# First mixer of a two-layer decoder: the solve's steps are placed at other places between the products, and the next group's mixes run beside them

## The chip, the core and the metric

The kernel runs on one core of one Trainium2 chip. Its time is the device time of one execution in microseconds (µs), and the number that stands for a kernel is the median of several executions. A core has five engines with a queue of their own each: TensorE (PE in the profile, its weight loads are PEld), VectorE (DVE), ScalarE (ACT), GpSimd (POOL) and SyncE (SP, which here only issues copies between memories). Each engine works through its queue in order and waits on semaphores that others raise.

## The reference, cut to what matters

Two layers, 256 positions, 2048 channels. The first layer's mixer is a gated delta rule with 32 value heads on 16 key heads of width 128; the change touches it alone.

```python
proj = x @ w_in                                   # 256 x 2048 by 2048 x 12352
qkv, z, a, b = split(proj)
q, k, v = split(silu(causal_dwconv(qkv, conv_w))) # 16, 16 and 32 heads of 128
q, k = l2norm(q) * 128**-0.5, l2norm(k)
beta, g = sigmoid(b), -exp(a_log) * softplus(a + dt_bias)
# per head, in chunks of 64: decay from the cumulated g
sol = triangular_solve(I + strict(kb @ k.T * decay), [v * beta, kb * exp(gc)])
# a scan over the chunks carries the state S
o = (q * exp(gc)) @ S + tri(q @ k.T * decay) @ v_new
o = o * rsqrt(mean(o**2) + eps) * norm_g * silu(z)
y = o.reshape(256, 4096) @ w_o
```

After it come a layer norm, a gated convolution block, a second norm, a gated side input, and the second layer with another mixer. All matrices are float32.

## The kernel before, in words

**Products.** Every large product takes float32 weights in tiles of 512 KB (`raw`, four buffers, issued by SP at L110). ACT rounds a tile to a shorter format (`hi`, L115) and DVE takes the rest (`lo`, L116), three buffers each. A product then needs three passes, of the rounded weights with both halves of the input and of the rest with the rounded input. Keys, queries and values come out transposed through `gemm_t_steps` (L148 for `hi`, L152 for `lo`, results in `mm_ps`): a tile is 8 products with `hi` and 8 with `lo`. The gate z comes from `gemm_steps` (L187, L190, L194, results in `b_ps`): a tile is 12 products.

**Groups.** The first mixer goes in eight groups of two key heads and four value heads. For a group the stream of products is 8 tiles of values, 8 tiles of the next group's keys and queries, and 8 tiles of the next group's z, 24 tiles in all. In the last group the output weights stand in for what no next group needs (`ahead`).

**Small work of a group.** Beside the stream, each group needs a row of small products in plain float32, which the profile lists as two passes each:

- `front`: the keys with themselves (`g_ps<-k`, L546 and L547, the first small work after a group's z). From them DVE makes `L` (L582), copies bring `L` to memory and back (`lt`, `ld`), POOL inverts the diagonal blocks with them. The masked products `gt` (L511) use the buffer of `L` again, so they wait until the copies `lt<-L` have landed.
- `solve`: forward substitution in four blocks (index b) for each half of the positions (a = 0, 1). A step is `l_ps` (L708, products with the blocks before), `ts` (L710, DVE), `y_ps` (L714), `ys` and four `u` (L716, L718, ACT). Between the halves stand `x_ps` (L695), a DVE step into `v` (L697) and the transposes `v_ps` (L668).
- `outputs`: `o_ps` (L732, L733), squares on ACT, a reciprocal root and the gate on DVE; its transposes `ot_ps` (L752) are put off through the list `rest`.
- `mixes`: the queries with the keys (`g_ps<-q,k`), `qd` and `qo` (L599, L600, DVE), sums `ss_ps` (L606) and scales `s_ps` (L612).

**What sets the order.** `solve`, `outputs` and `mixes` are generators. `finish` chains them and is kept in `self.inter`; the products of `gemm_t_steps` call `next(self.inter)` after every second `hi` row and at the end of each half tile, so 24 times in 8 tiles. `gemm_steps` calls it after every row of products too. A bare `yield` is thus a place between products. What is left of `self.inter` when it is needed is written out at once. The framework's scheduler then orders each engine's queue by its own estimate of when things are ready; a small product can so stand a few products away from where it was written. In PSUM two banks (`sp`) serve `g_ps`, `ss_ps`, `s_ps` and one half of `v_ps`, two more (`bk`) `l_ps`, `y_ps`, `x_ps`, `o_ps`, `ot_ps` and the other half; a bank is given out again when its readers are done.

Of the kernel before, what the change touches and what calls it, by code (L numbers as in the profile page):

```python
# [2 lines left out]

# [62 lines left out]
class Trunk:  # L66
# [382 lines left out]
    def gdn_groups(self, pool, gk, cw, ng, oT, load, gates, ahead):  # L449
# [12 lines left out]
        for pd in pads:  # L462
            nc.gpsimd.memset(pd[:, 0:3], 0.0)
        h4 = range(4)
        five = lambda ap: ap.rearrange("p (j r) t -> p j r t", r=2)

        def conv(n0, out):
# [126 lines left out]
        def mixes(s):  # L594
            q, k, dm = (s[x] for x in ("q", "k", "qd"))

            p1, p2 = gram(k, q)
            for a, ps in enumerate((p1, p2)):
                nc.vector.tensor_tensor(five(dm[:, a]), bcast(ps[:, :, 0:P], 2, 2), five(dm[:, a]), op=ALU.mult)  # L599
            nc.vector.tensor_tensor(five(s["qo"]), bcast(p1[:, :, P:S], 2, 2), five(s["qo"]), op=ALU.mult)  # L600
            yield

            pss = self.sp.tile([P, 4], F32, tag="sp", name="ss_ps")
            for h in range(2):
                for a in range(2):
                    nc.tensor.matmul(pss[:, 2 * h + a:][:, 0:1], s["sq"][:, h, a * P:(a + 1) * P],  # L606
                                     self.ones[:, 0:1], start=True, stop=True)
            xm = pool.tile([P, 4, 16], F32, tag="xm", name="xm")
            nc.vector.tensor_tensor(xm, bcast(s["x8"].rearrange("p q e -> p (q e)"), 4, 1), bcast(self.blk, 16, 2),
                                    op=ALU.mult)  # L610
            ps8 = self.sp.tile([P, 16, 4], F32, tag="sp", name="s8_ps")
            nc.tensor.matmul(ps8.rearrange("p e h -> p (e h)"), self.rep, xm.rearrange("p b e -> p (b e)"),  # L612
                             start=True, stop=True)
            xh = pool.tile([P, 16, 4], F32, tag="xm", name="xh")
            nc.vector.tensor_tensor(xh, ps8, bcast(self.blk, 16, 1), op=ALU.mult)
            s8 = s["s8"] = pool.tile([P, 4, 2, 2], F32, tag="s8", name="s8", bufs=2)
            nc.vector.tensor_reduce(s8.rearrange("p b q a -> p (b q a)"), xh, axis=mybir.AxisListType.X, op=ALU.add)
            wq = s["wq"] = pool.tile([P, 2, 2], F32, tag="wq", name="wq", bufs=2)
            nc.vector.tensor_scalar(wq.rearrange("p h a -> p (h a)"), pss, 4 * RMS_EPS, RMS_EPS * 128.0,
                                    op0=ALU.add, op1=ALU.mult)  # L620
            rr = pool.tile([P, 2, P], F32, tag="y0", name="rr")
            nc.sync.dma_start(out=rr, in_=bass.AP(tensor=s["rd"].tensor, offset=s["rd"].offset,
                                                  ap=[[0, P], [P, 2], [1, P]]))
            nc.vector.tensor_tensor(five(s["n21"]), bcast(rr, 2, 2), five(s["n21"]), op=ALU.mult)
# [51 lines left out]
        def zgate(s, rest):  # L676

            zs = s["zs"] = pool.tile([P, 2, 512], F32, tag="zs", name="zs", bufs=2)

            def done(a, ps):  # L680
                nc.scalar.activation(zs[:, a], ps, AF.Tanh, scale=0.5)
                nc.vector.scalar_tensor_tensor(zs[:, a], zs[:, a], 1.0, ps, op0=ALU.add, op1=ALU.mult)

            for j, _ in enumerate(self.gemm_steps(w_in, 8192 + 512 * s["g"], 512, lambda k: self.xT[:, k], KT, done)):
                if j > 4 and rest:
                    rest.pop(0)()

        def solve(s):
            u = s["u"] = pool.tile([P, 2, 4, P], F32, tag="u", name="u")
            bank = lambda name: self.sp.tile([P, P], F32, tag="bk", name=name)  # L690
            for a in range(2):
                if a:
                    ps = self.sp.tile([P, 4, 4, 32], F32, tag="bk", name="x_ps")
                    for h in h4:
                        nc.tensor.matmul(ps[:, :, h], u[:, 0, h], s["n21"][:, h].rearrange("p (b i) -> p b i", b=4),  # L695
                                         start=True, stop=True)
                    nc.vector.scalar_tensor_tensor(s["v1"], ps, -2.0, s["v1"], op0=ALU.mult, op1=ALU.add)  # L697
                    yield
                    yield
                    s["turn"](1)  # L700
                    yield
                y = pool.tile([P, 4, P], F32, tag="y", name="ys", bufs=2)
                for b in range(4):
                    r = s["vs"][:, b]
                    if b:
                        ps = bank("l_ps")
                        for c in range(b):
                            nc.tensor.matmul(ps, LB[:, a, pair(c, b)], y[:, c], start=not c, stop=c == b - 1)  # L708
                        r = pool.tile([P, P], F32, tag="ts", name="ts")
                        nc.vector.scalar_tensor_tensor(r, ps, s["s8"][:, b, 1, a:a + 1], s["vs"][:, b],  # L710
                                                       op0=ALU.mult, op1=ALU.add)
                        yield
                    ps = bank("y_ps")
                    nc.tensor.matmul(ps, pm[:, a, b], r, start=True, stop=True)  # L714
                    if b < 3:
                        nc.scalar.activation(y[:, b], ps, AF.Copy)  # L716
                    for h in h4:
                        nc.scalar.activation(u[32 * b:32 * b + 32, a, h], ps[32 * h:32 * h + 32], AF.Copy)  # L718
                    yield
                yield  # L720

        def outputs(s):

            g, u = s["g"], s["u"]
# [3 lines left out]
            for a in range(2):  # L728
# [8 lines left out]
                nc.vector.scalar_tensor_tensor(f[:, a], ss[:, a], 1.0 / 128, bcast(s["wq"][:, :, a], 2, 2),  # L737
                                               op0=ALU.mult, op1=ALU.add)
                parts.append(ps)
                yield  # L740
            fa = self.rsqrt(pool, f.rearrange("p a j r -> p (a j r)"), 8)

            def gate(a):
# [19 lines left out]

        def finish(s, n):

            yield
            yield from solve(s)
            yield from outputs(s)
            if n is not None:
                yield from mixes(n)  # L770

        def front(s):
            with self.tc.high_priority() if not s["g"] else ExitStack():
# [2 lines left out]
                blocks(s)  # L776
            causal(s)

        rest, s, last = [], keys(0), None
        for g in range(8):  # L780
            if g:
                self.inter = finish(last, s)
            turn = values(s)
            for _ in self.inter:
                pass
            rest.extend(turn)
            if not g:
                rest.insert(0, lambda: list(mixes(s)))
                zgate(s, rest)
            if g < 7:  # L790
                n = keys(g + 1, rest)
                zgate(n, [])
            else:
                ahead(6, rest)
            inverses(s)
            if g < 7:
                front(n)
                substitute(n)
                last, s = s, n
        self.inter = finish(s, None)  # L800
        ahead(4, ())
        for _ in self.inter:
            pass
        ahead(3, ())
        for turn in rest:
            turn()
# [435 lines left out]
```

## Time and profile before

| what | value |
|---|---|
| median of 3 runs | 2774.2 µs (2773.87 to 2776.98) |
| the profiled execution's own time | 2774.66 µs |
| its span in the profile | 2772.9 µs |
| PE busy, weight loads busy | 2745.8 µs (99%), 2351.3 µs (85%) |
| DVE, ACT, POOL busy | 1857.8 µs (67%), 1486.3 µs (54%), 344.0 µs (12%) |
| granted TensorE clock | 1.0 |
| DMA | 525.10 MB, mean 189 GB/s |
| first mixer, first to eighth group's start | 54.9 to 637.0 µs |

The profile comes from one execution. The span runs from the first to the last instruction of the program; the execution's own time has 1.8 µs around it. A row of a timeline has the start in µs from the span's start, the length in µs, the engine, the source line, the operation, output and inputs by the program's names, shapes and a count; in brackets stands how long the engine was idle before it and what ended that. A busy PE is not a PE at its peak: products overlap in the records, so what a wait costs is read from the distance between starts.

### The profile page before, as it was taken

The numbers are of one execution on the slowest core, as the hardware profiler recorded it, in microseconds if no ns is written. First come the engines' busy times: TensorE is split into PE (matmuls) and PEld (weight loads), VectorE is DVE, ScalarE is ACT, GpSimd is POOL, SyncE is SP. The second block draws the span as 40 slices with busy tenths as digits, with TensorE's granted clock in tenths as the row PEclk, the third lists the DMA queues.
The fourth block names the chain that finished last, engine by engine and source line by source line (L and its number), as shares of the span: only waits on it lengthen the run. The fifth ranks groups of instructions, "written<-read, shape, count | busy, mean of one in ns | idle before, by whom it ended". The sixth has DMA issues, their size and how long they took to land. (4 is left out here: it accounts for less than half of the span.)

```text
span 2772.9 us, 40054 instructions
## 1 busy us (share of the span) xinstructions
PE 2745.8 (99%) x14604; PEld 2351.3 (85%) x14604; DVE 1857.8 (67%) x3109; ACT 1486.3 (54%) x2512; POOL 344.0 (12%) x682
## 2 busy tenths in 40 slices
PE   8999999999999999999999999999999999999999
PEld 7888888888888888888888889888888888888887
DVE  7787788787556666666545766775666666655566
ACT  5676676776545555555434544455455555543444
POOL 1553334443100000000000000210000000000000
PEclk9999999999999999999999999999999999999999
DMA  7766676666575666666566567545566666655656
GB/s 227 206 166 176 165 186 172 185 168 160 180 233 163 186 209 204 208 199 206 193 195 207 181 185 232 175 144 165 175 190 197 197 190 195 198 193 192 211 171 193
DMA packets 435142, 525.10 MB, mean 189 GB/s; under 512 B 50976, under 2 KB 324496, under 8 KB 434688
## 3 DMA queue, kind: packets, MB, share of 16 engines
q1 hardware_dynamic: 427952, 504.05, 60.1%
q0 software_dynamic: 6992, 18.49, 2.6%
q8 instruction: 115, 1.88, 0.3%
q14 instruction: 83, 0.68, 0.1%
HBM read 516.62 MB, written 8.97 MB: 190 GB/s over the span
## 5 line engine op out<-in xcount | busy, mean ns | idle before, releaser
L116 DVE TENSOR_TENSOR lo<-raw,hi 128x1024 fp32r<-128x1024 f32 (+1 forms) x920 | 1125.2, 1224 | 617.8 <-ACT hi L115 602.7
L115 ACT ACTIVATE hi<-raw 128x1024 fp32r<-128x1024 f32 (+1 forms) x920 | 967.8, 1054 | 694.3 <-PE b_ps L190 428.4
L148 PE MATMUL mm_ps<-xT,hi 128*128 128x512 f32 (+1 forms) x4176 | 1042.5, 396 | 7.0 <-DVE xT L230 5.7
L148 PEld LDWEIGHTS mm_ps<-xT,hi 128*128 128x128 f32 (+1 forms) x4176 | 759.2, 189 | 151.6 <-ACT hi L229 5.6
L152 PE MATMUL mm_ps<-xT,lo 128*128 128x256 f32 (+1 forms) x4176 | 562.1, 284 | 1.7 <-DVE lo L116 1.7
L152 PEld LDWEIGHTS mm_ps<-xT,lo 128*128 128x128 f32 (+1 forms) x4176 | 540.9, 191 | 23.9 <-DVE lo L116 2.2
L187 PE MATMUL b_ps<-hi,xT 128*128 128x512 f32 (+1 forms) x704 | 270.1, 385 | 0.0
L190 PE MATMUL b_ps<-hi,xT 128*128 128x512 f32 (+1 forms) x704 | 268.4, 383 | 0.0
L225 ACT ACTIVATE fold<-mm_ps 128x256 f32<-128x256 f32 x261 | 97.5, 376 | 251.2 <-PE mm_ps L148 251.0
L187 PE MATMUL b_ps<-hi,hTA 128*128 128x512 f32 x512 | 199.2, 389 | 0.0
L190 PE MATMUL b_ps<-hi,hTA 128*128 128x512 f32 x512 | 199.2, 389 | 0.0
L194 PE MATMUL b_ps<-lo,xT 128*128 128x512 f32 (+1 forms) x704 | 188.2, 383 | 0.0
L244 POOL DMA_DIRECT2D lng<-in_ln_g x16 | 8.8, 551 | 1239.1 <-PE b_ps L194 654.0
L190 PEld LDWEIGHTS b_ps<-hi,xT 128*128 128x128 f32 x704 | 132.1, 188 | 24.9
L635 POOL TENSOR_TENSOR xt<-ld,xi 128x60 f32<-128x60 f32 (+24 forms) x248 | 113.3, 457 | 319.5 <-DMA ld<-lt 300.7
L187 PEld LDWEIGHTS b_ps<-hi,xT 128*128 128x128 f32 x704 | 132.1, 188 | 24.4
L194 PEld LDWEIGHTS b_ps<-lo,xT 128*128 128x128 f32 x704 | 130.2, 188 | 24.6
L194 PE MATMUL b_ps<-lo,hTA 128*128 128x512 f32 x512 | 136.8, 389 | 0.0
L637 POOL TENSOR_TENSOR xi<-xi,xt 128x60 f32<-128x60 f32 (+24 forms) x248 | 119.8, 483 | 19.4
L190 PEld LDWEIGHTS b_ps<-hi,hTA 128*128 128x128 f32 x512 | 96.1, 188 | 20.0
L194 PEld LDWEIGHTS b_ps<-lo,hTA 128*128 128x128 f32 x512 | 96.1, 188 | 20.0
L187 PEld LDWEIGHTS b_ps<-hi,hTA 128*128 128x128 f32 x512 | 96.1, 188 | 19.9
(264 smaller groups left out, 2579.5 us busy)
## 6 DMA issues: line engine op xcount, KB each, us to landing
raw<-in_gdn_w_in SPq DMA_DIRECT2D x192, 512.0 KB, 4.6
raw<-in_ffn_w_gate SPq DMA_DIRECT2D x160, 512.0 KB, 4.1
raw<-in_ffn_w_up SPq DMA_DIRECT2D x160, 512.0 KB, 4.4
raw<-in_ffn_w_down SPq DMA_DIRECT2D x160, 512.0 KB, 3.8
raw<-in_dsa_w_in SPq DMA_DIRECT2D x72, 512.0 KB, 3.7
raw<-in_gdn_w_o SPq DMA_DIRECT2D x64, 512.0 KB, 4.4
raw<-in_ple_w_gate SPq DMA_DIRECT2D x64, 512.0 KB, 4.6
raw<-in_dsa_w_o SPq DMA_DIRECT2D x32, 512.0 KB, 4.2
```

Of the source, the lines that this page charges most:

```text
L115: act = nc.scalar.activation(hi, raw, AF.Copy)
L116: ins = nc.vector.tensor_tensor(lo, raw, hi.bitcast(F32), op=ALU.subtract)
L148: ins = nc.tensor.matmul(q[:m, :], hi[:, k, o:o + m], x[:, k0 + k].rearrange("p a b -> p (a b)"), start=k0 + k == 0, stop=last)
L152: ins = nc.tensor.matmul(q[:m, S:], lo[:, k, o:o + m], x[:, k0 + k, 0, :], start=False, stop=last)
L187: ins = nc.tensor.matmul(ps[a][:, :n], xh, hi, start=k == 0, stop=False)
L190: self.before = nc.tensor.matmul(ps[a][:, :n], xl, hi, start=False, stop=False)
L194: self.last = nc.tensor.matmul(ps[a][:, :n], x(k)[:, 0, a * P:(a + 1) * P], lo, start=False, stop=k == kt - 1)
L225: nc.scalar.activation(t[:m], ps[:, S:], AF.Copy)
L244: ins = self.nc.gpsimd.dma_start(out=r, in_=bass.AP(tensor=src.tensor, offset=src.offset, ap=[[0, P], [1, n]]))
L635: nc.gpsimd.tensor_tensor(tmp[:, :m, :w], bcast(ld[:, i + 1:, i], m, 1), xi[:, :m, i:i + 1].to_broadcast([P, m, w]), op=ALU.mult)
L637: nc.gpsimd.tensor_tensor(xi[:, :m, i + 1:], xi[:, :m, i + 1:], tmp[:, :m, :w], op=ALU.subtract)
```

## The change

What it does: (1) every bare `yield` between two dependent steps of `solve`, and between the two halves of `outputs`, becomes two. (2) `finish` no longer chains `mixes` behind `outputs`: it advances both in turn, `mixes` starting after 14 places, and `mixes` pauses three places after its first part. (3) `self.inter` of a group is set at the end of the group's turn and is not written out after the values but after the next keys and queries, so it has 48 places in place of 24; in the last turn output tiles stand in for the keys. (4) The transposes in `rest` go beside the z products and no longer beside the keys. (5) In the first group z comes first and `mixes` is written out behind it at once. No instruction of the engines' arithmetic is added or taken away.

```diff
--- before.py
+++ after.py
@@ -1,3 +1,4 @@
+import itertools
 import math
 from contextlib import ExitStack
 
@@ -462,6 +463,7 @@
         for pd in pads:
             nc.gpsimd.memset(pd[:, 0:3], 0.0)
         h4 = range(4)
+        pause = lambda n: itertools.repeat(None, n)
         five = lambda ap: ap.rearrange("p (j r) t -> p j r t", r=2)
 
         def conv(n0, out):
@@ -598,7 +600,7 @@
             for a, ps in enumerate((p1, p2)):
                 nc.vector.tensor_tensor(five(dm[:, a]), bcast(ps[:, :, 0:P], 2, 2), five(dm[:, a]), op=ALU.mult)
             nc.vector.tensor_tensor(five(s["qo"]), bcast(p1[:, :, P:S], 2, 2), five(s["qo"]), op=ALU.mult)
-            yield
+            yield from pause(3)
 
             pss = self.sp.tile([P, 4], F32, tag="sp", name="ss_ps")
             for h in range(2):
@@ -682,7 +684,7 @@
                 nc.vector.scalar_tensor_tensor(zs[:, a], zs[:, a], 1.0, ps, op0=ALU.add, op1=ALU.mult)
 
             for j, _ in enumerate(self.gemm_steps(w_in, 8192 + 512 * s["g"], 512, lambda k: self.xT[:, k], KT, done)):
-                if j > 4 and rest:
+                if j and rest:
                     rest.pop(0)()
 
         def solve(s):
@@ -695,10 +697,9 @@
                         nc.tensor.matmul(ps[:, :, h], u[:, 0, h], s["n21"][:, h].rearrange("p (b i) -> p b i", b=4),
                                          start=True, stop=True)
                     nc.vector.scalar_tensor_tensor(s["v1"], ps, -2.0, s["v1"], op0=ALU.mult, op1=ALU.add)
-                    yield
-                    yield
+                    yield from pause(2)
                     s["turn"](1)
-                    yield
+                    yield from pause(2)
                 y = pool.tile([P, 4, P], F32, tag="y", name="ys", bufs=2)
                 for b in range(4):
                     r = s["vs"][:, b]
@@ -709,14 +710,14 @@
                         r = pool.tile([P, P], F32, tag="ts", name="ts")
                         nc.vector.scalar_tensor_tensor(r, ps, s["s8"][:, b, 1, a:a + 1], s["vs"][:, b],
                                                        op0=ALU.mult, op1=ALU.add)
-                        yield
+                        yield from pause(2)
                     ps = bank("y_ps")
                     nc.tensor.matmul(ps, pm[:, a, b], r, start=True, stop=True)
                     if b < 3:
                         nc.scalar.activation(y[:, b], ps, AF.Copy)
                     for h in h4:
                         nc.scalar.activation(u[32 * b:32 * b + 32, a, h], ps[32 * h:32 * h + 32], AF.Copy)
-                    yield
+                    yield from pause(2)
                 yield
 
         def outputs(s):
@@ -737,7 +738,7 @@
                 nc.vector.scalar_tensor_tensor(f[:, a], ss[:, a], 1.0 / 128, bcast(s["wq"][:, :, a], 2, 2),
                                                op0=ALU.mult, op1=ALU.add)
                 parts.append(ps)
-                yield
+                yield from pause(2)
             fa = self.rsqrt(pool, f.rearrange("p a j r -> p (a j r)"), 8)
 
             def gate(a):
@@ -763,11 +764,12 @@
 
         def finish(s, n):
 
-            yield
-            yield from solve(s)
-            yield from outputs(s)
+            steps = [itertools.chain(solve(s), outputs(s))]
             if n is not None:
-                yield from mixes(n)
+                steps.append(itertools.chain(pause(14), mixes(n)))
+            while steps:
+                yield
+                steps = [x for x in steps if next(x, steps) is not steps]
 
         def front(s):
             with self.tc.high_priority() if not s["g"] else ExitStack():
@@ -776,31 +778,36 @@
                 blocks(s)
             causal(s)
 
-        rest, s, last = [], keys(0), None
-        for g in range(8):
-            if g:
-                self.inter = finish(last, s)
-            turn = values(s)
+        def flush():
             for _ in self.inter:
                 pass
-            rest.extend(turn)
-            if not g:
-                rest.insert(0, lambda: list(mixes(s)))
-                zgate(s, rest)
+
+        rest, s = [], keys(0)
+        for g in range(8):
+            turn = values(s)
             if g < 7:
-                n = keys(g + 1, rest)
-                zgate(n, [])
+                if not g:
+                    zgate(s, [])
+                    for _ in mixes(s):
+                        pass
+                n = keys(g + 1)
+                flush()
+                rest.extend(turn)
+                zgate(n, rest)
             else:
-                ahead(6, rest)
+                ahead(3, ())
+                flush()
+                rest.extend(turn)
+                ahead(3, rest)
             inverses(s)
             if g < 7:
                 front(n)
                 substitute(n)
-                last, s = s, n
+                self.inter = finish(s, n)
+                s = n
         self.inter = finish(s, None)
         ahead(4, ())
-        for _ in self.inter:
-            pass
+        flush()
         ahead(3, ())
         for turn in rest:
             turn()
```

Three places where the queues now stand otherwise, shown for one group; the other middle groups read alike. Line numbers of the changed kernel are one or two higher than before.

PE, from the first half's solve on (`n_1490` is the buffer n21 of that group). Before:

```order
L148 MATMUL mm_ps<-xT,hi 128x512 x4
L708 MATMUL l_ps<-ys,LB 128x128 x3
L148 MATMUL mm_ps<-xT,hi 128x512 x4
L152 MATMUL mm_ps<-xT,lo 128x256 x16
L148 MATMUL mm_ps<-xT,hi 128x512 x6
L714 MATMUL y_ps<-ts,pm 128x128
L148 MATMUL mm_ps<-xT,hi 128x512 x2
L695 MATMUL x_ps<-n_1490,u 128x4x32 x3
L148 MATMUL mm_ps<-xT,hi 128x512 x3
L695 MATMUL x_ps<-n_1490,u 128x4x32
L148 MATMUL mm_ps<-xT,hi 128x512 x5
L152 MATMUL mm_ps<-xT,lo 128x256 x3
```

The same place now:

```order
L715 MATMUL y_ps<-ts,pm 128x128
L709 MATMUL l_ps<-ys,LB 128x128 x2
L149 MATMUL mm_ps<-xT,hi 128x512 x3
L709 MATMUL l_ps<-ys,LB 128x128
L149 MATMUL mm_ps<-xT,hi 128x512 x5
L153 MATMUL mm_ps<-xT,lo 128x256
L715 MATMUL y_ps<-ts,pm 128x128
L153 MATMUL mm_ps<-xT,lo 128x256 x15
L149 MATMUL mm_ps<-xT,hi 128x512 x4
L697 MATMUL x_ps<-n_1490,u 128x4x32 x2
L548 MATMUL g_ps<-q,k 128x256 x2
L549 MATMUL g_ps<-q,k 128x128 x2
```

The products between the last `y_ps` of the half and `x_ps` grew from 2 to 19, and `g_ps<-q,k`, which stood behind `o_ps`, now stands among the `x_ps`.

DVE, where `L` is made (the `ts` between them is the solve's). Before:

```order
L582 SCALAR_TENSOR_TENSOR L<-g_ps,c,L 128x128 x5
L116 TENSOR_TENSOR lo<-raw,hi 128x1024
L582 SCALAR_TENSOR_TENSOR L<-g_ps,c,L 128x128 x3
L503 TENSOR_TENSOR n_2478<-g_ps,qo 128x512
L116 TENSOR_TENSOR lo<-raw,hi 128x1024
```

Now:

```order
L584 SCALAR_TENSOR_TENSOR L<-g_ps,c,L 128x128 x3
L117 TENSOR_TENSOR lo<-raw,hi 128x1024
L584 SCALAR_TENSOR_TENSOR L<-g_ps,c,L 128x128 x4
L117 TENSOR_TENSOR lo<-raw,hi 128x1024
L584 SCALAR_TENSOR_TENSOR L<-g_ps,c,L 128x128
L505 TENSOR_TENSOR n_2478<-g_ps,qo 128x512
```

The eighth and last `L` now stands behind one more `lo`.

SP, the copies of the same stretch. Before:

```order
L110 DMA raw<-in_gdn_w_in 128x4x256
L587 DMA lt<-L 32x8x32 x4
L110 DMA raw<-in_gdn_w_in 128x4x256 x2
L591 DMA ld<-lt 32x1024 x4
L514 DMA lo<-gt 256x1x96
L514 DMA lo<-gt 256x1x64
L514 DMA lo<-gt 256x1x32
L110 DMA raw<-in_gdn_w_in 128x4x256 x3
L622 DMA rr<-rd 128x256
```

Now:

```order
L111 DMA raw<-in_gdn_w_in 128x4x256 x2
L589 DMA lt<-L 32x8x32 x4
L111 DMA raw<-in_gdn_w_in 128x4x256
L593 DMA ld<-lt 32x1024 x4
L516 DMA lo<-gt 256x1x96
L516 DMA lo<-gt 256x1x64
L516 DMA lo<-gt 256x1x32
L624 DMA rr<-rd 128x256
L111 DMA raw<-in_gdn_w_in 128x4x256 x5
```

A second weight tile now stands ahead of the four `lt<-L`, and `rr<-rd`, which waits for `ss_ps`, stands ahead of three more weight tiles.

## The prediction

> **What bounds the kernel now.** I read the page first, then PE's waits, then PE's timeline of one group.
>
> ```profile
> span 2772.9 us, 40054 instructions
> PE 2745.8 (99%) x14604; PEld 2351.3 (85%) x14604; DVE 1857.8 (67%) x3109; ACT 1486.3 (54%) x2512; POOL 344.0 (12%) x682
> PE y_ps L714 <- DVE ts L710: 3.4, 6, 0.9
> PE g_ps L546 <- DVE gt L511: 2.9, 1, 2.9
> PE x_ps L695 <- ACT u L718: 1.4, 7, 0.2
> PE ss_ps L606 <- DVE qd L599: 1.0, 5, 0.2
> ```
>
> PE's queue is the path: it is hardly ever idle, and listed waits of the first mixer come to 8.7 µs. That list understates, since a product's record covers part of a wait. So I count a group by starts. The pace of the stream, of a z tile, and of small products without a wait:
>
> ```profile
> 2013.43 3.65 PE mm_ps L148 x16
> 2017.08 1.91 PE mm_ps L152 x16
> ...
> 130.26 0.39 PE L187 MATMUL b_ps<-hi,xT 128*128 128x512 f32 x1
> 132.98 0.39 PE L187 MATMUL b_ps<-hi,xT 128*128 128x512 f32 x1
> ...
> 167.68 0.38 PE L732 MATMUL o_ps<-u,qo 128*128 128x128 f32 x2
> 167.90 0.39 PE L733 MATMUL o_ps<-u,qd 128*128 128x128 f32 x2
> ...
> 135.71 0.59 PE L546 MATMUL g_ps<-k 128*128 128x256 f32 x2
> 219.91 0.59 PE L546 MATMUL g_ps<-k 128*128 128x256 f32 x2
> 636.97 0.38 PE L546 MATMUL g_ps<-k 128*128 128x256 f32 x1
> ```
>
> A `hi` product takes 3.65/16 = 0.228 µs, a `lo` product 1.91/16 = 0.119, a transposed tile (8 of each) 2.78, a z tile (12 products from start to start) 2.72, a small pass 0.11. A group is 16 × 2.78 + 8 × 2.72 = 66.2 µs of stream. Its small work is 98 passes (y 16, l 24, x 8, v 8, o 24, ss 8, s 2, ot 8) × 0.11 = 10.8, and two grams of about 1.3 each (`g_ps<-k` starts at 219.91, its eight passes include four wide ones). Floor: 79.7 µs. Measured: (636.97 − 135.71)/6 = 83.5 a group. So **3.8 µs a group** is waiting and the weight loads that a wait uncovers; seven groups (1 to 7) hold 27 µs, 1.0% of the kernel, and that is the most that any placing of this work can win there. Where it sits, group 2:
>
> ```profile
> 235.30 1.07 PE L695 MATMUL x_ps<-n,u 128*128 128x128 f32 x6
> 237.26 0.49 PE L695 MATMUL x_ps<-n,u 128*128 128x128 f32 x2 [0.19 <-ACT u L718]
> 239.10 0.60 PE L668 MATMUL v_ps<-ident,v 128*128 128x128 f32 x4
> 240.31 0.49 PE L714 MATMUL y_ps<-vs,pm 128*128 128x128 f32 x2
> 241.35 0.40 PE L708 MATMUL l_ps<-ys,LB 128*128 128x128 f32 x2
> 243.31 0.46 PE L714 MATMUL y_ps<-ts,pm 128*128 128x128 f32 x2 [0.17 <-DVE ts L710]
> 246.34 0.38 PE L714 MATMUL y_ps<-ts,pm 128*128 128x128 f32 x2
> 247.46 0.49 PE L708 MATMUL l_ps<-ys,LB 128*128 128x128 f32 x2
> 253.87 0.59 PE L546 MATMUL g_ps<-q,k 128*128 128x256 f32 x2
> 256.98 1.05 PE L606 MATMUL ss_ps<-cst,sq 128*128 128x1 f32 x8
> 722.13 1.05 PE L695 MATMUL x_ps<-n,u 128*128 128x128 f32 x8
> ```
>
> Between the two `x_ps` rows stand 6 passes and 3 products, 0.66 + 0.68 = 1.34; they start 1.96 apart: 0.6 lost. From l at 241.35 to y at 243.31 stand two passes, two `lo` and five `hi`, 1.6: 0.4 lost. From y at 246.34 to l at 247.46 six passes and one product, 0.9: 0.2, and 0.1 more for the bare weight load. `ss_ps` loses 0.2. The last group, with wider gaps, has its `x_ps` in one piece.
>
> **Part by part: what the wider places win.** Nearly every dependent step of the solve now has 1.6 to 3.7 µs of stream before it, where it had 0.2 to 1.8. A step needs its DVE or ACT work (0.35 and 0.28 by the rows of `ts` and `ys`), and at worst one `lo` of 1.23 or one `hi` of 1.06 ahead of it: about 1.6 to 1.8. So most waits go. Two keep their short gap: `y_ps` behind `v_ps` (two passes and 0.57 of stream, 0.60 before; from 239.10 to 240.31 it took 1.21 for 1.04) stays at 0.3 with the bare load, and one `l_ps` stands three products, 0.68, behind its `y_ps`; with a `hi` ahead of `ys` I take 0.5 for it. For all other places 0.4 together. That leaves 1.2 of 3.8, a gain of 2.6 a group if nothing new came.
>
> **What the earlier mixes cost.** `g_ps<-q,k` needs both `sp` banks, which hold the keys' gram until `gt` has read it. It stood at 34 µs after the group's start (253.87 − 219.91), long after `gt`. Now it stands behind 44 `hi` and 48 `lo` products (10.0 + 5.7), the keys' gram (1.3) and 24 passes (2.6): 19.7 µs, with the 0.5 above 20.2. When is `gt` read?
>
> ```profile
> 230.82 0.86 DVE L582 SCALAR_TENSOR_TENSOR L<-g_ps,c,L 128x128 f32<-128x128 f32 x3
> 232.55 1.23 DVE L116 TENSOR_TENSOR lo<-raw,hi 128x1024 fp32r<-128x1024 f32 x1 [0.27 <-ACT hi L115]
> 239.82 1.29 DVE L511 TENSOR_TENSOR gt<-g_ps,qd 128x512 f32<-128x512 f32 x2 [1.05 <-DMA lt<-L]
> ...
> 230.94 0.37 SPq L110 DMA_DIRECT2D raw<-in_gdn_w_in  x1
> 231.72 1.81 SPq L587 DMA_DIRECT2D lt<-L  x4
> 233.81 0.39 SPq L110 DMA_DIRECT2D raw<-in_gdn_w_in  x1
> ...
> 82.18 1.29 DVE L511 TENSOR_TENSOR gt<-g_ps,qd 128x512 f32<-128x512 f32 x2
> 83.02 0.67 PE L546 MATMUL g_ps<-q,k 128*128 128x256 f32 x2 [2.85 <-DVE gt L511]
> ```
>
> The last `L` ends at 231.68, 11.8 after the start; SP issues `lt` at once; `gt` starts 8.1 after the first issue, at 19.9, held by the landing. In the changed order one more `lo` (1.23) stands ahead of the last `L` and one `ts` (0.35) moves behind it: 12.6. The second weight tile, which SP now issues ahead of `lt`, waits for that `lo` and takes 0.4 to issue: `lt` at 12.8. With the same 8.1, `gt` starts at 20.9, and by the first group's rows `g_ps` follows 0.84 later: **21.7**. PE, there at 20.2, waits 1.5. Here nothing hides it: behind `g_ps` in PE's queue stands the whole stream. DVE's queue behind `gt` holds conv steps and two `lo` tiles that PE needs several µs later, so they add nothing at this size.
>
> The wait itself the trace can't show, only its parts. From below: single copies of `lt` landed in 3.3 to 8.1 µs, median 5.0. With 5.0 after the fourth issue (12.8 + 1.4), `gt` starts at 19.2 and PE waits nothing. From above: a weight tile that lands alone takes 3.9, and if `lt` waits for all of it the wait is 5.4.
>
> ```profile
> DMA to landing us min/median/max: 3.3/5.0/8.1
> DMA to landing us min/median/max: 3.9/3.9/3.9
> DMA to landing us min/median/max: 8.0/8.0/8.0
> DMA to landing us min/median/max: 6.6/7.1/7.4
> ```
>
> (All `lt` copies; the weight tile at 225.8; the one at 230.9; the four `lt` at 231.7.) I take 1.5, because in this row a tile issued 0.8 ahead landed with `lt`, and both then shared what the new tile would share.
>
> The Trainium skill, in DMA: Bandwidth & Descriptors, section Queues, rings and completion order, says that copies issued by SP go through one ring on each DMA engine and that a ring's entries are taken in order. By that rule `lt` starts moving only when the tile ahead has been taken from the ring, and the sum would be that of the late-landing rival below. The trace doesn't contradict it: the tile at 230.9 and the four `lt` behind it landed almost together, 8.0 and 6.6 to 7.4 after their issues.
>
> **Other parts.** The first group: its `mixes` now stand behind the whole z, when `gt` is long done: −2.9 (the listed wait). The last group's solve needs some 40 places, and what `ahead` has left falls short: the second half's last steps are written out with 0 to 0.9 µs between them, where they had 0.9 without a wait. Four such steps at about 0.3 (the l step above): +1.2. Moved `ot_ps` and `v_ps` (12 passes) have 2.7 between them, as before: 0. On SP, `rr<-rd` now holds three weight tiles until `ss_ps` is done, about 2 µs longer than `lo<-gt` held them; SP was already held longer by `LB` later in the group, without a PE wait: 0.
>
> **Sum.** A group keeps 1.2 + 1.5 = 2.7 of 3.8: −1.1, seven groups −7.7; first group −2.9; last +1.2: −9.4 µs. The profiled execution took 2774.66 (span 2772.9 and 1.8 around it), 0.5 over the median of 2774.2. So 2774.2 − 9.4 = **2765 µs**.
>
> **Rivals.** *No new wait* (0.2): `lt` lands in 6.5 or less, `g_ps` finds `gt` done. For it: the longest part of 8.1 is shared with a tile, and that tile is now issued 0.9 earlier relative to the group. Against it: the extra tile. Seven groups × −2.6, −2.9, +1.2 = −20: 2754. *`lt` lands late, slower* (0.12): the second tile is served whole ahead of `lt`, +3.9. The wait becomes 5.4, a group loses 2.8, seven 19.6, with −2.9 and +1.2: +18, 2792. The point of turning: a wait of 2.8 a group brings 2774, 3.6 brings slower by 0.2%. Against it: DVE's gap before `gt` was 1.05 with a tile in front already. *DVE fills up* (0.18): the solve's second half and the squares now run beside the next keys, where DVE has no room.
>
> ```profile
> 281.50:292.00 10.50, 10.50 (x48) 8.69 (x47) 10.46 (x24) 10.00 (x22) 3.05 (x6) 1.00 0.74 208
> ...
> PE mm_ps L152 <- DVE lo L116: 1.7, 2, 1.4
> ```
>
> DVE was busy 10.46 of 10.50 µs there, and a late `lo` has cost PE 1.4 once. One such wait a group is 9.8 and takes the gain away: 2775. Against it: PE did not wait in that very window, as `lo` has three buffers, and the mixes' three long steps leave this stretch.
>
> **How the numbers follow.** The forecast (0.5) spans waits of 0.7 to 2.3, 2759 to 2771. A measurement of this kernel can tell about 0.2%, 5.5 µs, from no change. Faster by more: nearly nine tenths of the forecast and the no-wait rival, 0.63. Within: the rest of the forecast and DVE's rival, 0.23. Slower: the late landing and a part of DVE's, 0.14. The range of 8 in 10 reaches from the no-wait case to just beyond DVE's: 2752 to 2777.
>
> **What would show it.** Right: PE's list of waits has `g_ps` behind `gt` in seven groups, near 1.5 each by starts; `x_ps` and the `y_ps` and `l_ps` of the second half without brackets; groups near 82.4 µs; the first group without its 2.85. Wrong: `g_ps` without a wait and groups near 81; or `gt` starting after 22 µs; or new waits of L153 for `lo`.

## The result, and the profile after

The changed kernel takes **2789.6 µs** (median of 6 runs, 2787.9 to 2792.1), the kernel before on the same chip 2776.4 (6 runs, 2773.9 to 2777.4): a ratio of 1.0051, with a 95% interval of 1.0038 to 1.0064. It is slower by half a per cent, where the prediction had 2765 and faster.

The head of the changed kernel's page, and PE's longest waits in the first mixer (µs in total, times, longest):

```profile
span 2786.7 us, 40040 instructions
PE 2744.8 (98%) x14604; PEld 2357.0 (85%) x14604; DVE 1863.3 (67%) x3109; ACT 1485.2 (53%) x2512; POOL 340.4 (12%) x682
...
PE g_ps L548 <- DVE gt L513: 18.1, 7, 3.8
PE ss_ps L608 <- DVE qd L601: 2.5, 1, 2.5
PE y_ps L715 <- DVE ts L711: 2.1, 8, 0.3
PE y_ps L715 <- ACT hi L116: 1.4, 5, 0.3
PE mm_ps L153 <- DVE lo L117: 1.3, 1, 1.3
```

The span grew by 13.8 µs: 10.7 in groups 1 to 6, 2.5 in the first group and 1.0 from the last group's start on, less 0.3 by which the first group starts earlier. `x_ps` is gone from the list, as forecast. In place of the small waits stands one large one, `g_ps` behind `gt`, in all seven groups. The starts of groups 1 and 7 in PE's timeline:

```profile
137.86 0.59 PE L548 MATMUL g_ps<-k 128*128 128x256 f32 x2
...
649.86 0.59 PE L548 MATMUL g_ps<-k 128*128 128x256 f32 x2
```

A group takes (649.86 − 137.86)/6 = 85.3 µs; it took 83.5 before, and 82.4 was forecast. One group's wait, followed back over three engines (group 3, which starts at 309.99):

```profile
322.86 5.58 SPq L589 DMA_DIRECT2D lt<-L  x4
...
332.48 1.29 DVE L513 TENSOR_TENSOR gt<-g_ps,qd 128x512 f32<-128x512 f32 x2 [2.71 <-DMA lt<-L]
...
333.32 1.10 PE L548 MATMUL g_ps<-q,k 128*128 128x256 f32 x4 [2.99 <-DVE gt L513]
```

SP begins to issue `lt` 12.87 after the group's start (12.8 was forecast), but the four issues take 5.58 instead of 1.81; `gt` starts at 22.5 (20.9 forecast; after 22 was a sign of being wrong), and PE stands idle for 3.

There is a second loss that no list of waits shows: **the granted clock**. Four stretches of the changed kernel, 3.41 µs each, two and two in succession (columns: busy µs of PE, PEld, DVE, ACT, POOL, then PE's clock, DMA share, GB/s):

```profile
157.39:160.81 3.42, 0.81 (x6) 0.57 (x4) 0.18 (x1) 0.67 (x3) 0.00 (x0) 1.00 0.78 223
160.81:164.22 3.41, 2.23 (x6) 1.91 (x7) 2.24 (x6) 0.00 (x0) 0.00 (x0) 0.50 0.60 160
331.45:334.86 3.41, 1.54 (x10) 1.47 (x11) 2.38 (x6) 0.00 (x0) 0.00 (x0) 1.00 0.64 181
334.86:338.27 3.41, 3.41 (x23) 3.02 (x22) 3.14 (x6) 1.46 (x3) 1.06 (x3) 1.00 0.46 111
```

Group 1's wait left PE busy for 0.81 of 3.42 µs, and the next stretch ran at half clock. Group 3's wait left 1.54, and the clock stayed. In the first mixer the clock is at half from 92.5 to 96.0, 160.8 to 167.6, 502.1 to 505.6 and 672.8 to 676.2 µs: 17.1 µs, of which at most half, 8.5, is lost (PE was not busy in all of it, as in the second row). The kernel before has no such stretch in its profile. The mean clock of whole executions agrees: 0.995 to 0.997 in the changed kernel's six, 0.998 to 1.0 in the seventeen of the kernel before that were run beside E5 to E7.

### The profile page after: what moved, and what is told of

Its sections match the earlier page's. It is cut to its first block, busy times and chain, and to the rows that moved or that the text cites. A ratio compares the mean times of both kernels' runs of the same rounds, so it can differ in the third digit from the quotient of the medians.

```text
span 2786.7 us, 40040 instructions
## 1 busy us (share of the span) xinstructions
PE 2744.8 (98%) x14604; PEld 2357.0 (85%) x14604; DVE 1863.3 (67%) x3109; ACT 1485.2 (53%) x2512; POOL 340.4 (12%) x682
## 5 line engine op out<-in xcount | busy, mean ns | idle before, releaser
L188 PEld LDWEIGHTS b_ps<-hi,xT 128*128 128x128 f32 x704 | 132.1, 188 | 23.9
L639 POOL TENSOR_TENSOR xi<-xi,xt 128x60 f32<-128x60 f32 (+24 forms) x248 | 111.3, 449 | 19.4
```

What stands on the lines that cost most here:

```text
L188: ins = nc.tensor.matmul(ps[a][:, :n], xh, hi, start=k == 0, stop=False)
L639: nc.gpsimd.tensor_tensor(xi[:, :m, i + 1:], xi[:, :m, i + 1:], tmp[:, :m, :w], op=ALU.subtract)
```

## The experiments

All times are medians in µs; ratios are to the kernel before on the same chip, with 95% intervals. The experiments ran on four chips; there the kernel before took 2775.2 to 2776.2, so times of two chips can be compared to about 1 µs. "Group" is the mean of groups 1 to 6 from the starts of `g_ps<-k`, "first" the length of group 0, "waits" PE's listed waits for `gt` and `v`, "half" the time at half clock in the first mixer; these four are from each profiled execution.

| kernel | time | ratio | group | first | waits | half |
|---|---|---|---|---|---|---|
| before | 2776 | – | 83.5 | 80.9 | 2.9 | 0 |
| the change | 2789.6 | 1.0051 (1.0038–1.0064) | 85.3 | 83.4 | 18.1 | 17.1 |
| E1 late mixes | 2783.4 | 1.0021 (1.0012–1.0031) | 84.3 | 83.6 | 16.0 | 17.1 |
| E2 first group as before | 2785.2 | 1.0032 (1.0020–1.0043) | 84.2 | 81.8 | 17.9 | 10.2 |
| E3 both | 2782.2 | 1.0023 (1.0013–1.0032) | 83.6 | 83.9 | 16.3 | 13.7 |
| E4 wait filled | 2780.6 | 1.0017 (1.0009–1.0026) | 84.0 | 82.9 | 3.2 | 3.4 |
| E5 `gt` behind `v` | 2759.0 | 0.9940 (0.9928–0.9952) | 80.9 | 82.3 | 0 | 3.4 |
| E6 first group in two | 2759.0 | 0.9940 (0.9928–0.9953) | 81.0 | 82.2 | 0.6 | 3.4 |
| E7 wide places alone | 2777.0 | 1.0004 (0.9996–1.0013) | 84.6 | 84.0 | 19.6 | 23.9 |
| E8 `gt` behind `v`, early mixes | 2767.1 | 0.9968 (0.9958–0.9979) | 82.4 | 85.3 | 3.8 | 6.8 |
| E9 first group beside keys | 2756.2 | 0.9931 (0.9918–0.9945) | 80.9 | 80.2 | 0 | 3.4 |
| E10 `rd` behind `ld` | 2767.0 | 0.9970 (0.9958–0.9981) | 82.3 | 82.3 | 0 | 3.4 |
| E11 the same, late mixes | 2756.0 | 0.9934 (0.9921–0.9948) | 81.1 | 78.9 | 0 | 0 |
| E12 E9 and E10 | 2757.6 | 0.9935 (0.9923–0.9948) | 81.0 | 78.6 | 0 | 0 |

**E1. Is it the early place of the mixes?**

```
-                steps.append(itertools.chain(pause(14), mixes(n)))
+                steps.append(itertools.chain(pause(24), mixes(n)))
```

> The change with one number altered: the mixes of the next group begin ten places later (pause(24) for pause(14)), behind the second half's second y_ps. Theory A (the loss is PE's wait for gt at g_ps<-q,k, 18.1 us in 7 groups, and the half clock that follows some of those waits, 13.7 us of it in groups 1, 5 and 7, so 6.8 us lost): gt begins 21.1 to 23.3 us into a group, g_ps now comes about 35 us into it, so the row for g_ps in the list of waits goes and no record at half clock is left but group 0's: 2789.6 - 18.1 - 6.8 = 2765 (2760 to 2772). Rival B (the group is bound by something else, DVE or the weight tiles, and the wait only shows it first): the time stays at 2782 or more and the idle time turns up at another product of the solve or at a weight tile.

Measured: 2783.4. Theory A fell: three quarters of the gain it had promised did not come. Time and sign are those of rival B, the idle time at another product of the solve. PE's waits, and the stretch behind `gt` on DVE and PE in group 3:

```profile
PE v_ps L670 <- DVE v L699: 16.0, 7, 3.4
...
329.11 1.29 DVE L513 TENSOR_TENSOR gt<-g_ps,qd 128x512 f32<-128x512 f32 x2 [2.49 <-DMA lt<-L]
331.12 0.68 DVE L699 SCALAR_TENSOR_TENSOR v<-x_ps,v 128x512 f32<-128x512 f32 x1
...
331.85 0.66 PE L670 MATMUL v_ps<-ident,v 128*128 128x128 f32 x4 [2.30 <-DVE v L699]
```

`g_ps` no longer waits, but `v_ps` does, for almost as long. DVE's queue stands still at `gt` until `lt` lands, and `v<-x_ps` of the running solve is behind it. In the kernel before, the narrow places put it ahead (DVE's timeline, the same group):

```profile
321.25 0.68 DVE L697 SCALAR_TENSOR_TENSOR v<-x_ps,v 128x512 f32<-128x512 f32 x1
323.41 1.29 DVE L511 TENSOR_TENSOR gt<-g_ps,qd 128x512 f32<-128x512 f32 x2 [1.48 <-DMA lt<-L]
```

DVE stood still there too, for 1.48 µs, but nothing that PE wanted soon was behind it. That is theory D: the loss is a queue that stands still, and the wider places moved a needed step behind it.

**E2 and E3. The first group.**

```
                 if not g:
-                    zgate(s, [])
-                    for _ in mixes(s):
-                        pass
+                    rest.extend([lambda: None] * 4 + [lambda: list(mixes(s))] + turn)
+                    zgate(s, rest)
```

> The change with the first group's mixes put back inside its z product, where they were before; all else as changed. Theory A (in the first group the earlier place costs 2.5 us: ss_ps waits 2.47 us for qd, and the clock is at half for 3.4 us): 2789.6 - 2.5 = 2787 (2785 to 2789). The prediction's own step had this edit win 2.9 us, by which the time would be 2792.5.

> Both edits: mixes ten places later and the first group as before. Theory A: 2765 - 2.5 = 2762 (2757 to 2770), no record at half clock inside the span, and below the kernel before by about 14 us. Rival B: 2780 or more.

Measured: E2 2785.2, in its range and 7 below what the prediction's step would give: the first group's new place costs, it does not win. Of the 4.4 below the change, the first group itself has 1.6 in the profiles; the groups behind it, whose order on PE and DVE is the same, have the rest, with other stretches at half clock. The first group's wait in the changed kernel, on PE:

```profile
91.72 1.15 PE L608 MATMUL ss_ps<-cst,sq 128*128 128x1 f32 x8 [2.47 <-DVE qd L601]
```

`g_ps` finds `gt` done there, but `ss_ps` follows at once and waits for `qd` on DVE instead, and half clock follows that. E3 came out at 2782.2, not at 2762, for E1's reason: `v_ps` waits 12.9 µs in it, and the clock falls in groups 1 and 2.

**E4. What halves the clock?** Sixteen transposes that compute nothing keep PE at work during most of each wait.

```
+        def fill(steps):
+            ps = self.sp.tile([P, 4, P], F32, tag="bk", name="fill_ps")
+            for i in range(16):
+                nc.tensor.transpose(ps[:, i % 4], self.ident, self.ident)
+            yield from steps
...
-                steps.append(itertools.chain(pause(14), mixes(n)))
+                steps.append(itertools.chain(pause(15), fill(mixes(n))))
```

> The change with 16 transposes of the identity, written to a bank that nobody reads, ahead of each later group's g_ps<-q,k, which starts one place later (pause(15)): TensorE is busy for 1.74 us of each wait (16 x 0.109, by v_ps<-ident,v), and all of x_ps, not half of it, stands ahead of g_ps. g_ps still starts when gt is done, so the waits' length in time is not altered by more than x_ps's half, 0.6 us in six of seven groups (3.6 us). Theory A (the clock halves because TensorE was idle for most of one 3.41 us stretch): the records at half clock in groups 1, 5 and 7 go, another 6.8 us: 2789.6 - 3.6 - 6.8 = 2779 (2776 to 2782), group 0's record stays. Rival C (the clock falls for another reason, such as load or lateness, and not for want of work on TensorE): the records stay and the time is 2786 (2784 to 2790).

Measured: 2780.6. Half clock is gone from groups 1, 5 and 7, and only group 0's is left; the mean clock of the twelve executions is 0.998 to 0.999, against 0.995 to 0.997. Useless work in the wait made the kernel 9 µs faster, so idleness of PE, and not the lateness of the data, is what brings the half clock. Up to 3.6 of the 9 would by the expectation come from starting one place later; that place without the transposes was not run.

**E5 and E6. `gt` behind `v<-x_ps`.** Taking E1, the `gt` part of `causal`, with the copies `lo<-gt`, becomes a function of its own that runs in the solve's later steps, and is tied behind `v<-x_ps`:

```
+            ins = nc.vector.tensor_tensor(five(gt[:, a]), ...)
+            if x:
+                self.after(ins, x)
...
+        def later(s, n):
+            yield from pause(18)
+            scale(n, s["x"])
+            yield from pause(6)
+            yield from mixes(n)
```

In E6 the first group's mixes also run in two pieces, beside the sixth and seventh places of its z.

> As the run with the late mixes (2783.4 us), and VectorE's two gt products, which wait for the landing of lt<-L, are put behind v<-x_ps of the running solve on VectorE's queue instead of ahead of it; g_ps<-q,k keeps its late place. Theory D (the loss is VectorE's queue standing still at gt until lt lands, 21 to 23 us into a group; whatever stands behind it on VectorE and is wanted by TensorE then makes TensorE wait: g_ps in the change, v_ps<-v with the late mixes): the 16.0 us of v_ps waits and the half clock behind them (13.7 us of records in groups 1, 5 and 7, 6.8 us lost) go: 2783.4 - 16.0 - 6.8 = 2760.5 (2755 to 2768). Rival B (the group is bound by something else): the idle time moves on to a third product and the time stays over 2775.

> The same, and the first group's mixes run in two pieces beside the sixth and seventh places of its z product, neither at the place before nor behind the whole z. Theory D: gt of group 0 starts 26.8 to 27.9 us into the group and is done at 28.1 to 29.2; g_ps comes at about 28.6 to 29, and ss_ps one z tile (2.8 us) later, when qd is done: neither the 2.5 to 3.4 us wait of g_ps nor the 2.5 us wait of ss_ps, and no half clock there (1.7 us): 2760.5 - 2.5 - 1.7 = 2756 (2751 to 2764). Rival: one of the two waits is still there, and the time is that of the run before this one, within 2 us.

Measured: E5 **2759.0**, and its list has no wait for `gt` or `v` left. DVE and PE in group 3, and the starts of groups 1 and 7:

```profile
319.75 0.68 DVE L705 SCALAR_TENSOR_TENSOR v<-x_ps,v 128x512 f32<-128x512 f32 x1
320.75 1.28 DVE L519 TENSOR_TENSOR gt<-g_ps,qd 128x512 f32<-128x512 f32 x2
...
321.29 0.60 PE L676 MATMUL v_ps<-ident,v 128*128 128x128 f32 x4
...
136.95 0.59 PE L554 MATMUL g_ps<-k 128*128 128x256 f32 x2
622.54 0.59 PE L554 MATMUL g_ps<-k 128*128 128x256 f32 x2
```

A group takes (622.54 − 136.95)/6 = 80.9 µs, as much as the prediction's floor of 79.7 and the 1.2 it left. Theory D holds; rival B, a bound elsewhere, does not. E6 won nothing over E5, as its rival had it: `ss_ps` still waits 1.9 in the first group.

**E7. The wider places alone**: the mixes run behind the outputs again, the first group as in E2.

```
-            steps = [itertools.chain(solve(s), outputs(s))]
-            if n is not None:
-                steps.append(itertools.chain(pause(14), mixes(n)))
+            steps = [itertools.chain(solve(s), outputs(s), mixes(n) if n is not None else ())]
```

> Of the change only the wider places: the next group's mixes run after the outputs again, as before the change, and the first group's mixes are where they were before. Theory D: the wider places push x_ps of the solve so late that v<-x_ps on VectorE stands behind gt, so v_ps waits about 2.2 us in each of 7 groups, as in the run with late mixes and the first group as before (2782.2): 2782 (2778 to 2786), slower than before although no product is moved ahead. The prediction's own steps (wider places win 2.6 us in each of 7 groups, only the earlier mixes cost) give 2776.4 - 18 = 2758.

Measured: 2777.0, from 2771.9 to 2783.5, the same as before. The wait is where theory D puts it:

```profile
PE v_ps L670 <- DVE v L699: 16.3, 7, 2.9
```

The 18 µs that the wider places were to win are not there, with no product moved ahead. The median is 1 under theory D's range; the profiled execution was this kernel's slowest, with 23.9 µs at half clock and a mean clock of 0.995, while the two fastest of its twelve runs, 2771.9 and 2773.3, had 0.998 and 0.999.

**E8. `gt` behind `v`, but early mixes** (E5 with `pause(15)` and no second pause).

> The change with gt behind v<-x_ps on VectorE's queue, but with the mixes early (one place later than in the change, behind x_ps and eight of the next passes). Theory D (the order on VectorE's queue is the cause, not the mixes' early place as such): v<-x_ps no longer waits behind gt, gt is done about 23.2 us into the group, g_ps<-q,k comes at about 24, so neither waits for long: under 1 us a group, and no half clock in groups 1 to 7: 2759 + 0 to 5 = 2759 to 2764. Rival E (the early place itself costs, because gt cannot be done in time whatever stands ahead of it): g_ps waits 2 us or more in each group and the time is 2775 to 2790, as in the change.

Measured: 2767.1, between the two ranges, nearer to D. Of PE's waits:

```profile
PE g_ps L554 <- DVE gt L519: 3.8, 4, 1.7
PE y_ps L721 <- DVE ts L717: 2.1, 7, 0.4
PE y_ps L721 <- ACT hi L116: 1.7, 6, 0.3
```

`g_ps` is nearly free, so the early place as such was not the large loss. It is not free either: the second half's `y_ps` waits are those of the changed kernel, and they are gone in E5. A group is 1.4 µs longer than with late mixes. The profile is that of the slowest of E8's seven executions. Its first group is 3.0 longer too, with PE and DVE in the order of E5: a late `lo` costs 2.8 there, 1.2 in E5.

**E9. The first group's mixes beside the next keys** (E5 with one more edit):

```
-                    for _ in mixes(s):
-                        pass
+                    self.inter = mixes(s)
```

> As the run with gt behind v<-x_ps and late mixes (2759.0), and the first group's mixes run between the products of the next keys and queries, a place apart, instead of in one piece ahead of them. Theory: the first group's loss left in that run, the wait of ss_ps for qd (1.5 us in its profile), the half clock behind it (3.4 us at half, so 1.7) and the wait for a weight tile held up behind rr<-rd (1.2), comes from ss_ps standing one product behind g_ps: 2759.0 - 3 to 4.4 = 2755 (2752 to 2757), group 0 at about 78 us. Rival: the first group's DVE queue is full there whatever the spacing, the wait moves to s_ps or v_ps, and the time stays at 2758 to 2760.

Measured: 2756.2. The first group falls from 82.3 to 80.2, two µs short of the forecast, since `ss_ps` still waits 0.8 and one stretch at half clock is left.

**E10 to E12. Why does `lt` land so late?** In the changed kernel, group 3, SP's transfers in the order of their issue (number, duration in ns, first and last start; below each its time from issue to landing): `rd<-rs`, the two weight tiles, and two of the four `lt`.

```profile
L576 SPq DMA_DIRECT2D rd<-rs x1: 366/366/366, 317.5 to 317.5; - x1
DMA to landing us min/median/max: 8.6/8.6/8.6
...
L111 SPq DMA_DIRECT2D raw<-in_gdn_w_in x1: 368/368/368, 320.0 to 320.0; - x1
DMA to landing us min/median/max: 10.1/10.1/10.1
...
L111 SPq DMA_DIRECT2D raw<-in_gdn_w_in x1: 367/367/367, 322.4 to 322.4; - x1
DMA to landing us min/median/max: 9.2/9.2/9.2
...
L589 SPq DMA_DIRECT2D lt<-L x2: 498/2272/4047, 322.9 to 323.4; - x2
DMA to landing us min/median/max: 8.6/8.8/8.9
```

They land at 326.1, 330.1, 331.6 and from 331.8 on: in the order of issue, although a tile that lands alone takes 3.9 (the row for 225.8 in the prediction). The first in the row is `rd`, 256 elements of 4 bytes. The kernel before had it at the same place, and as slow (group 3, 7.5 µs after the group's start):

```profile
L574 SPq DMA_DIRECT2D rd<-rs x1: 367/367/367, 310.6 to 310.6; - x1
DMA to landing us min/median/max: 8.8/8.8/8.8
```

E10 moves this copy, and nothing else:

```
+            rd = s["rd"] = self.dr.tile([2, P], F32, tag="rd", name="rd")
+            self.after(nc.sync.dma_start(out=rd.rearrange("j p -> p j"),
+                                         in_=s["rk"].rearrange("p (j a) -> p a j", a=2)[:, 1]), last)
```

(in `blocks`, behind the last `ld<-lt`, and no longer in `sums`). E11 adds `pause(24)` and E9's first group; E12 is E9 with this move.

> The change with one copy moved on SP: rd<-rs, 256 elements of 4 bytes, issued behind ld<-lt instead of ahead of two weight tiles and lt<-L; PE's and VectorE's order is the change's. In the change, group 3, rd is issued 7.5 us after the group's start and lands at 16.2, a weight tile issued at 10.0 lands at 20.1, the next, issued at 12.5, at 21.6, and lt, issued from 12.9 on, at 21.8 to 22.4. Theory F (rd's many small writes hold up whatever SP issues behind it, because the transfers of a queue land in order): without rd ahead the tiles land some 4.3 us after their issue, lt at 18 to 19, gt starts near 19, g_ps<-q,k (20.2) finds it done: the 18.1 us of waits and the 6.8 us of half clock in groups 1, 5 and 7 go: 2789.6 - 24.9 = 2765 (2760 to 2771), with no edit of PE's or VectorE's order. Rival G (rd is slow but holds up nothing, lt is late for the two weight tiles ahead of it): lt lands at 21 or later as before, 2786 to 2792.

> The same move of rd, with the mixes ten places later and the first group's mixes beside the next keys; gt stays where the change has it on VectorE's queue, ahead of v<-x_ps. Theory F: gt no longer stands still for lt, so v_ps<-v does not wait (it waited 16.0 us with the late mixes and rd ahead): the time of the run with gt behind v<-x_ps and the same first group, 2756 (2752 to 2761). Rival G: v_ps waits as with the late mixes, 2778 to 2783.

> The run with gt behind v<-x_ps, late mixes and the first group's mixes beside the next keys (2756.2), and rd behind ld as well. No wait for gt or v is left there, so theory F leaves nothing for it to win: 2756 (2754 to 2757). Rival: at its new place rd holds up the weight tiles behind it and PE waits for one: 2758 or more.

Measured: 2767.0, **2756.0** and 2757.6. E10 and E11 are where theory F had them; E12 is 0.6 above its range, just short of its rival's 2758, and its list has one wait of 1.5 for a copy, `pm<-tt`. E10's weight tiles (the two still issued ahead of `lt` and two more), `lt`, `rd` and `lo` in group 3:

```profile
L111 SPq DMA_DIRECT2D raw<-in_gdn_w_in x4: 367/368/389, 307.6 to 317.9; - x4
DMA to landing us min/median/max: 3.8/3.9/4.2
...
L588 SPq DMA_DIRECT2D lt<-L x4: 444/450/497, 314.5 to 316.0; - x4
DMA to landing us min/median/max: 3.2/3.2/3.5
...
L595 SPq DMA_DIRECT2D rd<-rs x1: 426/426/426, 321.2 to 321.2; - x1
DMA to landing us min/median/max: 8.1/8.1/8.1
...
L516 SPq DMA_DIRECT2D lo<-gt x3: 556/611/617, 322.6 to 323.8; - x3
DMA to landing us min/median/max: 7.3/7.8/8.2
```

`lt` now lands in 3.2 to 3.5 µs, and its four issues are not held, although two weight tiles stand ahead of it as in the changed kernel, 10.0 and 12.5 after the group's start. So rival G is out. The lateness went to the copies that are now behind `rd`: `lo` takes 7.3 to 8.2, and PE's list has no wait for them. One copy of 1 KB moved on SP's queue takes off 22.6 µs. PE's order is the changed kernel's, but that one `y_ps` a group stands three products earlier; on DVE `gt`, `v` and `qd<-g_ps` keep their order, while conv steps, `lo` tiles and some scalings change places. The prediction drew on the Trainium skill, DMA: Bandwidth & Descriptors, section Queues, rings and completion order, for the rule that a ring's entries are taken in order. These runs agree, with `lt` at 8.6 to 8.9 µs behind `rd` and 3.2 to 3.5 ahead of it.

E11 needs no split of `causal` and beats both kernels, 20 µs under the one before; E9 and E12 can't be told from it. What stays between E10 and E11, 11.0 µs, is about the early mixes' 1.2 a group and the first group's 3.4.

## Why the prediction was wrong, point by point

The forecast was −9.4 µs; the two profiled spans differ by +13.8. The step that failed is the cost of the earlier mixes, in the landing of `lt`; a term for half clock was missing. The 23 µs between them, by its own steps:

- **What the wider places win**: right as a size, 2.6 a group between the kernel before and E5, and `x_ps` left the list of waits. The gain showed only where `gt` did not stand in its way: E7, without the early mixes, won nothing. No run has the wider places alone with `gt` out of the way, so that all 2.6 come from them is argued.
- **What the earlier mixes cost**: the place was right (`g_ps` behind `gt` behind the landing of `lt`, in seven groups), the size was not. The step forecast 1.5 µs a group, as "a tile issued 0.8 ahead landed with `lt`, and both then shared what the new tile would share". It measured 18.1/7 = 2.6: 7.7 µs more. In group 3 the 8.1 from the first issue of `lt` to `gt`, which the step carried over, became 9.6. Nothing was shared: all land one behind the other, behind `rd`, which the step does not mention although the kernel before shows it (8.8 above); with `rd` moved, E10 has no wait of `g_ps` left. The rival in which `lt` lands late came nearest, 2792, by luck: it was right that `lt` waits for what stands ahead, but it took the second tile for the cause, and in E10 that tile is still there. Its wait of 5.4 a group was twice the measured one; half clock and the first group filled most of the difference.
- **The bound from below** of that step was misread. "All `lt` copies", 3.3 to 8.1 with median 5.0, holds the copies `ld<-lt` as well; the copies `lt<-L` alone took 4.5 to 8.1, median 6.9, in the kernel before:

```profile
L587 SPq DMA_DIRECT2D lt<-L x32: 327/450/2848, 73.7 to 650.5; - x32
DMA to landing us min/median/max: 4.5/6.9/8.1
```

With 6.9 after the fourth issue `gt` starts at 21.1 and not at 19.2, so the case without a wait, and the chance of 0.2 for it, stood on too little.

- **The sum** had no term for half clock: up to 8.5 µs. Its waits were priced at their length. E4 shows the missing term.
- **The first group**, −2.9: wrong in sign, +2.5. The step took away `g_ps`' wait, and the next one was late: `ss_ps` for `qd`, 2.47, and half clock behind it (1.7 of the 8.5).
- "DVE's queue behind `gt` … so they add nothing at this size": the sentence looked at conv steps and `lo` tiles and missed `v<-x_ps`. In the changed kernel `g_ps` waits first and hides this; E1 uncovered it, at 16.0 µs.
- **The second half's `y_ps`**, part of the 0.4 "for all other places": listed waits of 3.5 µs in all. E8 and E10 keep them and E5 and E11 do not, so they come with the early mixes' DVE work. What is left of the difference, 23.2 − 7.7 − 8.5 − 3.7 (the first group's 5.4 without its half clock) = 3.3 µs, about fits them; it was not taken apart further.
- **The last group**, +1.2: from its start to the first `n_ps` of the layer norm it took 231.4 µs before and 232.4 in the changed kernel, with a wait and half clock in it; no run takes the term apart.
- `rr<-rd` on SP, priced 0: in the first group one `lo` came 1.3 late for PE behind the tiles it held; in groups 1 to 7 no such wait is listed.

## What to carry to other kernels

A step on an in-order queue that waits for a transfer is a gate for everything behind it: before spreading work out, list which steps will cross that gate, since widening the gaps can lose more than it wins without moving a product ahead. Ask also what sets the transfer's landing: here a copy of 256 single elements, needed by nobody soon, took over 8 µs to land and made a critical copy behind it land some 5 µs later. Moving it took off 22.6 µs, where the change had added 13.3. A wait of 2 to 4 µs on TensorE has to be priced with the 3.4 or 6.8 µs at half clock that can follow it.

## What the runs showed of the hardware that was not expected

**Half clock comes by a fixed raster**, a grid in time. All stretches at half clock in the first mixers are 3.41 or 6.83 µs long and begin at whole multiples of 3.413 µs from the start of the clock's record. In groups 1 to 7 of the fourteen profiles the clock falls where PE was busy for 0.49 to 1.42 µs of the raster stretch before, and nowhere behind one with 1.54 or more. The closest pair, from E7:

```profile
583.56:586.97 3.41, 1.42 (x9) 1.21 (x9) 3.37 (x9) 0.95 (x4) 0.00 (x0) 1.00 0.80 201
586.97:590.38 3.41, 3.41 (x18) 3.29 (x17) 2.34 (x4) 2.80 (x9) 2.74 (x6) 0.50 0.67 177
...
668.89:672.30 3.41, 1.54 (x9) 1.36 (x10) 3.37 (x8) 0.85 (x4) 0.19 (x1) 1.00 0.72 202
672.30:675.71 3.41, 3.41 (x27) 3.19 (x26) 2.20 (x5) 2.81 (x9) 2.94 (x7) 1.00 0.78 208
```

So a wait costs its own length in one group and 1.7 µs more in the next, by where it falls on the raster: by the starts, a wait of 2.4 µs halved the clock in the changed kernel's group 7, one of 3.2 in its group 3 did not. Once at half, a stretch that was busy for 2.23 µs (160.81 to 164.22 above) was followed by another at half; in the fourteen profiles this holds for 2.22 to 2.74 µs, and behind 3.18 the clock was full again. In group 0 four falls came behind stretches with 1.55 to 2.6 µs busy; all four hold `ss_ps`, whose passes are one column wide, so a record's busy time may overstate the work there. That is argued, not shown. The Trainium skill, TensorE: Matmul & The Clock Gate, section The HAM clock gate (the "warmup" mystery), has a free-running window of 3413 ns, which agrees with the raster. Its rule, in section HAM oscillation — how this bites in real kernels, that idle gaps over about 3.4 µs are the ones to avoid is too mild for these runs: here a gap of 2.6 µs (`v_ps` in E1's group 7) sufficed.

**Kernels with much half clock also spread more.** E7's twelve runs lie 11.6 µs apart, with mean clocks from 0.995 to 0.999, and E3's eleven 14.4, with 0.994 to 0.998; the seventeen of the kernel before on E7's chip lie 6.6 apart, with 0.998 to 1.0. In the fourteen profiles the clock's record, and with it the raster, starts 8.3 to 12.1 µs into the span, so its position against the program differs. That this makes the spread fits but was not tried.
